# Scan products F, G and X as 64x64 quarters of the TensorE array

## The chip, the cores and the metric

The kernel runs on one core of one Trainium2 chip. Its engines work side by side and are tied together by semaphores: TensorE (PE: matmuls, with weight loads listed as PEld), VectorE (DVE), ScalarE (ACT), GpSimd (POOL) and SyncE (SP, which issues most DMAs). Each engine takes its instructions in order. The metric is the device time of one execution in microseconds; lower is better.

## The reference, cut to what matters

One layer of a bidirectional RWKV-7 / short-convolution hybrid: 128 context tokens and 2048 latent tokens, 1024 channels, one input and one output projection. The part that the change touches is the RWKV-7 state recurrence, 8 heads of 64 channels, run once forward and once backward:

```python
def step(S, inp):
    r_t, w_t, k_t, v_t, kk_t, a_t = inp
    s_kk = jnp.einsum('bdhij,bdhj->bdhi', S, kk_t)
    S = (S * w_t[..., None, :] - s_kk[..., :, None] * (kk_t * a_t)[..., None, :]
         + v_t[..., :, None] * k_t[..., None, :])
    return S, jnp.einsum('bdhij,bdhj->bdhi', S, r_t)

s_final, ys = lax.scan(step, s0.astype(f32), xs)
```

The kernel does not step token by token. It cuts the tokens into chunks of 64; within a chunk the recurrence becomes products of 64x64 matrices (one per head and direction), one of which needs a triangular inverse, and only one state of 64x64 goes from chunk to chunk.

## The kernel before

**Phases.** `phase1` normalises, projects, and writes to DRAM the scaled operands of the scan: per direction four arrays (called al, rh, ka, be in `OPS`) of 512 channels by 2176 tokens. `phase2` is the scan. `phase3` makes the output projection; part of it (`ahead`) runs inside the last scan stages.

**Stages.** `stages` has 17 entries (`NST`). A stage is two groups, `st.g[0]` the forward and `st.g[1]` the backward direction, each of 8 units; a unit is one chunk of 64 tokens of two heads (128 partitions: head 0 on partitions 0 to 63, head 1 on 64 to 127). The two heads of a unit have the same channels' place, but separate 64x64 matrices.

**Parts of a stage**, each a Python generator that emits instructions:

- `partL` (L853): loads the operands `rr` [128, 5, 8, 64] of both directions on SP's queue, two DMAs for each. Slot 2 of `rr` holds a constant identity. `rr` comes from a ring of two buffers.
- `partM` (L871), for one direction after the other: `make_bd` (L829) copies `rr` slot 0 and slot 4 into block-diagonal operands `pb` and `qb` (four ScalarE copies of 64x512). `product` (L888) makes four units' matmuls into one PSUM bank of the pool `O.pm` (two banks, tag "m") and evicts it on VectorE with a mask (L893). F and f are the two halves of the first product (slot 0 against slots 2 and 3), G and g those of the second (slot 4 against slots 1 and 0), Q the transposes of slot 4. The block-diagonal operand lets a 128x128 matmul treat both heads at once; the zeros in it keep them apart. D (`blocks`) takes 32x32 blocks out of GA with ScalarE and VectorE and sends them to DRAM (`at`) from ScalarE's queue.
- `partI` (L909): GpSimd loads `at` as `ab` (issued by SP), inverts the 32x32 triangular blocks by a loop of 15 rounds (L931, L934), and writes the result `zt` to DRAM (L935).
- `partW` (L955): copies and loads that fill the stacked operands `lt` and `rt`; loads `zt` back as `zc`. `partU` (L981): finishes the 64x64 inverse from the 32x32 blocks by products of 32x32 pieces (`psU` L992, `psW` L999) and builds `zb`, again block-diagonal, 128 wide.
- `partB` (L1011): X is `zb` against F (`psX`, L1018, pool `O.p2`, two banks, tag "s"), copied with a minus sign into `lt`/`rt` by ScalarE; then E is `lt` against `rt` (`psE`, L1029) with a mask on VectorE.
- `partS` (L1034): the chain itself, 8 steps: two matmuls a direction (`psS`, L1054), then VectorE scales the state into the next unit's `sv` (L1067).

**Order.** `main` (L1159) interleaves them: in stage s the steps of `partS(s)` are the frame; between them come pieces of W, U and B of stage s+1 (by `ORDER`) and pieces of `partM(s+3)` (`LA` = 3 stages ahead; by the tuple at L1204). `MORD` says which products make up one piece of `partM`. At the end of a stage come `partL(s+4)` and `partI(s+3)`. The tile framework then orders the instructions of each engine by a simulated time line, so that the order on the chip can differ from the order of emission; tiles of one tag share buffers in turn.

Of the kernel before, what the change touches and what calls it, by code (L numbers as in the profile page):

```python
# [681 lines left out]
MORD = ("Ff", "GgD", "", "Q")  # L682
# [8 lines left out]
def phase2(K):  # L691
# [4 lines left out]
    B = Ctx()  # L696
# [38 lines left out]
    def setup_rest():  # L735
# [21 lines left out]
        B.zb = O.l1.tile([128, 2, 8, 128], F32, name="zb")  # L757
# [113 lines left out]
    def partM(s, st):  # L871

        at = S["at"][s]
        for gi, g in enumerate(st.g):
            d = g.d
            rr = g.rr
# [5 lines left out]
            def transposes():  # L882
                pq = O.pm.tile([128, 4, 128], F32, tag="m", name=f"psQ{s}_{gi}")
                for k in range(4):
                    T.transpose(pq[:, k, :], rr[:, 4, 2 * k:2 * k + 2, :].rearrange("p u t -> p (u t)"), B.idt[:])
                copy("q", g.Q, pq[:])

            def product(h, dst, w, x, mask, nm):  # L888
                ps = O.pm.tile([128, 4, 128], F32, tag="m", name=f"ps{nm}{s}_{gi}_{h}")
                for i in range(4):  # L890
                    u = h * 4 + i
                    T.matmul(ps[:, i, :].rearrange("p (a b) -> p a b", b=64), w[:, u, :], x[:, :, u, :], start=True, stop=True)  # L892
                V.tensor_tensor(dst[:, h * 4:h * 4 + 4, :], ps[:], mask.unsqueeze(1).broadcast_to((128, 4, 128)), ALU.mult)  # L893

            def blocks():
# [7 lines left out]
            ops = dict(Q=transposes, F=lambda: F(0), f=lambda: F(1), G=lambda: GA(0), g=lambda: GA(1), D=blocks)  # L903
            for piece in MORD:
                for c in piece:
                    ops[c]()
                yield
# [47 lines left out]
    def partW(s, st):  # L955
# [5 lines left out]
        for n in range(2):  # L961
            for g in st.g:
# [18 lines left out]
    def partU(s, st):  # L981
# [7 lines left out]
        rows = [(slice(sl * 64, sl * 64 + 32), slice(sl * 64 + 32, sl * 64 + 64)) for sl in range(2)]  # L989
        for u in range(16):  # L990
            for r0, r1 in rows:
                T.matmul(pu[r1, u, :], st.g[u // 8].GA[r0, u % 8, 96:128], st.zr[r0, u, :], start=True, stop=True)  # L992
        for r0, r1 in rows:
# [3 lines left out]
        for u in range(16):  # L997
            for r0, r1 in rows:
                T.matmul(pw[r0, u, :], B.bu[r1, u, :], st.zc[r1, u, :], start=True, stop=True)  # L999
        zf = B.zb[:].rearrange("p d u c -> p (d u) c")  # L1000
        for r0, r1 in rows:
# [9 lines left out]
    def partB(s, st):  # L1011
        for n in range(2):
            for gi, g in enumerate(st.g):
                us = half(g, n)
                g.E.append(tl([128, 4, 2, 128], "E", 4))
                px = O.p2.tile([128, 4, 128], F32, tag="s", name=f"psX{s}_{gi}_{n}")
                for i in range(4):
                    T.matmul(px[:, i, :], B.zb[:, gi, us.start + i, :], g.F[:, us.start + i, :], start=True, stop=True)  # L1018
                for hd in range(2):
                    copy("x" if hd else "y", g.fs[64:128, :, hd, us], px[64 - hd * 64:128 - hd * 64].rearrange("p u (b t) -> p b u t", b=2), True)  # L1020
# [138 lines left out]
    def main():  # L1159
# [12 lines left out]
        for s in range(NST):  # L1172
# [30 lines left out]
            for i, _ in enumerate(partS(s, st, sts.get(s + 1))):  # L1203
                for _ in range((2, 2, 2, 1, 1, 0, 0, 0)[i]):  # L1204
# [209 lines left out]
```

## Time and profile before

| | us |
|---|---|
| time, median of 3 runs (lowest to highest) | 1759.63 (1756.57 to 1762.25) |
| span of the profiled execution | 1752.9 |
| first psS product of the scan, in that span | 1034.2 |
| last F product | 1458.6 |
| last X product | 1560.3 |

The profile gives one execution's span from its first to its last instruction; no separate device time of that execution is kept, so its span stands beside the median of the runs. Rows of groups read: line, engine, operation, output<-inputs, shape, xcount | busy us, mean ns of one | idle us of the engine just before, and what ended most of it. Matmul records carry the array rows*columns in use in front of the shape. A row of a time line reads: start us, length us, engine, line, operation, tiles, count, and in brackets the idle time ahead of it with what ended it.

### The profile page before, as it was taken

To read this page: it belongs to the slowest core of one execution; us is meant where nothing else is said; L and a number is where in the kernel's file an instruction comes from. 1 tells how busy PE (TensorE), PEld (TensorE's weight loads), DVE (VectorE), ACT (ScalarE), POOL (GpSimd) and SP (SyncE) were. 2 spreads that over 40 slices of the span, in tenths; PEclk is the share of its full clock that TensorE was granted. 3 is DMA by queue.
4 is the path that set the end of the run, shared out by engine and by line. 5 is a ranking of instruction groups with operands and counts; after the bars stand their busy time and mean duration, and the time that the engine had idled before them with its cause. 6 is when DMAs were issued, how large, how long until landed. Compare 5 with 4: busy or idle time off the path is not lost. (4 is left out here: it accounts for less than half of the span.)

```text
span 1752.9 us, 33041 instructions
## 1 busy us (share of the span) xinstructions
PE 1647.9 (94%) x12400; PEld 1558.8 (89%) x12400; DVE 1093.0 (62%) x2092; ACT 870.1 (50%) x1719; POOL 582.1 (33%) x1089
## 2 busy tenths in 40 slices
PE   5999899998999999999998989999999999899998
PEld 2889898998999998999998979899999999787886
DVE  5875788866567766567764544475776666656333
ACT  4534455534143433334442367687788787633222
POOL 0011111111011101011120587777777778223221
PEclk9899999999999999999999998899999999999999
DMA  9797778785557646477666585587677875746442
GB/s 367 208 234 220 233 241 246 232 255 151 148 160 227 169 147 174 135 258 217 195 214 225 173 196 135 141 192 187 174 198 189 191 185 120 180 151 206 151 144 90
DMA packets 315825, 335.69 MB, mean 192 GB/s; under 512 B 166985, under 2 KB 263881, under 8 KB 301585
## 3 DMA queue, kind: packets, MB, share of 16 engines
q1 hardware_dynamic: 243360, 324.52, 62.6%
q10 hardware_dynamic: 70944, 4.60, 2.9%
q0 software_dynamic: 1360, 4.46, 0.7%
q8 instruction: 98, 1.61, 0.4%
q14 instruction: 63, 0.51, 0.1%
HBM read 221.42 MB, written 112.08 MB: 190 GB/s over the span
## 5 line engine op out<-in xcount | busy, mean ns | idle before, releaser
L934 POOL TENSOR_TENSOR zt<-zt,ztmp 128x30 f32<-128x30 f32 (+7 forms) x510 | 197.3, 387 | 39.3
L1054 PE MATMUL psS<-sv,E 128*128 128x64 f32 x1088 | 155.1, 277 | 1.0 <-DVE sv L1067 0.6
L1029 PE MATMUL psE<-str,stl 128*128 128x128 f32 x1088 | 144.1, 281 | 11.3 <-DVE E L1030 7.0
L1054 PEld LDWEIGHTS psS<-sv,E 128*128 128x128 f32 x1088 | 145.4, 200 | 3.3 <-DVE sv L1067 0.8
L1029 PEld LDWEIGHTS psE<-str,stl 128*128 128x128 f32 x1088 | 131.8, 194 | 14.1 <-DVE E L1030 7.9
L931 POOL TENSOR_TENSOR ztmp<-ab,zt 128x60 f32<-128x60 f32 (+7 forms) x255 | 130.8, 513 | 19.2
L1067 DVE TENSOR_TENSOR sv<-psS,pc 64x128 f32<-64x128 f32 x254 | 69.2, 277 | 92.9 <-PE psS L1054 92.2
L779 ACT COPY bd<-rr 64x512 f32<-64x512 f32 x136 | 84.0, 617 | 75.7 <-DMA rr<-scr_ops 23.3
L323 POOL TENSOR_TENSOR shk<-rawl 128x384 f32<-128x384 f32 (+1 forms) x24 | 20.7, 861 | 291.9 <-ACT rawl L319 291.9
L1030 DVE TENSOR_TENSOR E<-psE,msk 128x512 f32<-128x512 f32 x136 | 92.7, 684 | 33.0 <-PE psE L1029 32.3
L892 PE MATMUL psF<-rr,bd 128*128 128x128 f32 x544 | 80.0, 295 | 16.2 <-ACT Q L779 9.8
L892 PEld LDWEIGHTS psF<-rr,bd 128*128 128x128 f32 x544 | 70.7, 203 | 20.4 <-ACT Q L779 12.9
L1350 POOL TENSOR_TENSOR z<-z,x 128x512 f32<-128x512 f32 x32 | 43.6, 1364 | 126.6 <-DVE z L1346 105.9
L1018 PE MATMUL psX<-F,zb 128*128 128x128 f32 x544 | 78.2, 297 | 3.2 <-ACT zb L777 2.3
L197 POOL TENSOR_TENSOR hslb<-kd,hshb 128x384 fp32r<-128x384 f32 (+1 forms) x24 | 26.7, 1113 | 164.0 <-ACT hshb L196 143.5
L160 PE MATMUL mmc<-h,w 128*128 128x384 f32 (+1 forms) x192 | 67.9, 354 | 13.4 <-ACT q1r L321 9.8
L323 POOL TENSOR_TENSOR shv<-rawl 128x384 f32<-128x384 f32 (+1 forms) x24 | 25.4, 1060 | 153.4 <-ACT rawl L319 153.4
L892 PE MATMUL psG<-rr,bd 128*128 128x128 f32 x544 | 72.0, 280 | 4.4 <-DVE F L893 4.4
L1018 PEld LDWEIGHTS psX<-F,zb 128*128 128x128 f32 x544 | 71.6, 209 | 4.0 <-POOL zt L934 1.9
L892 PEld LDWEIGHTS psG<-rr,bd 128*128 128x128 f32 x544 | 65.7, 193 | 5.0 <-DVE F L893 4.8
L161 PE MATMUL mmc<-h,w 128*128 128x384 f32 (+1 forms) x192 | 66.1, 344 | 0.0
L162 PE MATMUL mmc<-h,w 128*128 128x384 f32 (+1 forms) x192 | 65.7, 342 | 0.0
(307 smaller groups left out, 5205.4 us busy)
## 6 DMA issues: line engine op xcount, KB each, us to landing
w<-scr_wsp SPq DMA_DIRECT2D x68, 1024.0 KB, 7.3
scr_wsp<-w SPq DMA_DIRECT2D x34, 1024.0 KB, 6.0
rr<-scr_ops SPq DMA_DIRECT2D x64, 512.0 KB, 4.6
scr_ops<-sp SPq DMA_DIRECT2D x160, 192.0 KB, 5.2
wr<-in_win SPq DMA_DIRECT2D x34, 512.0 KB, 6.3
ab<-scr_at SPq DMA_DIRECT2D x34, 256.0 KB, 4.2
x<-in_x SPq DMA_DIRECT2D x17, 512.0 KB, 3.8
wadas<-in_wada SPq DMA_DIRECT2D x8, 1024.0 KB, 13.0
```

The costliest lines, as they stand in the source:

```text
L160: T.matmul(ps[:, :n], w[:, 0, k], hh[:, 0, k, :n], start=k == 0, stop=False)
L161: T.matmul(ps[:, :n], w[:, 0, k], hh[:, 1, k, :n], start=False, stop=False)
L162: T.matmul(ps[:, :n], w[:, 1, k], hh[:, 0, k, :n], start=False, stop=k == 7)
L779: (V.tensor_copy if k in ON_DVE else P.copy)(dst, src)
L892: T.matmul(ps[:, i, :].rearrange("p (a b) -> p a b", b=64), w[:, u, :], x[:, :, u, :], start=True, stop=True)
L931: G.tensor_tensor(tv, ab[:, j:j + 2, j + 2:32].unsqueeze(1).broadcast_to((128, kn, 2, n)), zt[:, :kn, j:j + 2].unsqueeze(3).broadcast_to(( ...
L934: G.tensor_tensor(zt[:, :kn, j + 2:32], zt[:, :kn, j + 2:32], tv[:, :, r], ALU.subtract)
L1018: T.matmul(px[:, i, :], B.zb[:, gi, us.start + i, :], g.F[:, us.start + i, :], start=True, stop=True)
L1029: T.matmul(pe[:, i, hd, :].rearrange("p (b t) -> p b t", b=2), g.lt[:, :, hd, us.start + k + i].rearrange("p b t -> p (b t)"), g.rt[:, :, ...
L1030: V.tensor_tensor(g.E[n][:, k:k + 2].rearrange("p a b c -> p (a b) c"), pe[:].rearrange("p a b c -> p (a b) c"), B.msk[:, ME[g.d]].unsquee ...
L1054: T.matmul(sp[gi][:, q, hd, :], g.E[n][:, k, hd, :], sv[:, u, hd, :], start=True, stop=True)
L1067: r = V.tensor_tensor(dst, sp[gi][0:64, q], B.pc[0:64, d, 2 * p:2 * p + 2, c:c + 1].broadcast_to((64, 2, 64)), ALU.mult)
```

## The change

F, G and X are no longer made with 128x128 operands. Each product of a unit is now two matmuls with 64 rows and 64 columns of the array, one per head, and the products of both directions are emitted alternately, so that four consecutive matmuls take the four 64x64 quarters. `place` says into which half of the partitions a head's result goes: crossed for the forward direction, as it was, and straight for the backward one. The two directions write two PSUM banks. The ring `bd`, `make_bd` and their copies are removed; `rr` gets a third buffer; `zb` becomes half as wide. `MORD` has six pieces for both directions together (there were four for each), with D following the second half of G for both directions and the two Q at the end; the pieces go one to each of the first six steps.

```diff
-MORD = ("Ff", "GgD", "", "Q")
+MORD = ("F", "f", "G", "gD", "Q", "q")
...
-        B.bd = ring(O.r1, 2, [128, 8, 128], "bd", zero)
-        B.rr = ring(O.r1, 2, [128, 5, 8, 64], "rr", presetR)
+        B.rr = ring(O.r1, 3, [128, 5, 8, 64], "rr", presetR)
...
-        B.zb = O.l1.tile([128, 2, 8, 128], F32, name="zb")
+        B.zb = O.l1.tile([128, 2, 8, 64], F32, name="zb")
...
-    def make_bd(t_, src):
-        copy("b", t_[0:64, :, 64:128], src[0:64])
-        copy("c", t_[64:128, :, 0:64], src[64:128])
+    def place(g, hd):
+
+        return 1 - hd if g.d == 0 else hd
+
+    def rows(i):
+        return slice(i * 64, i * 64 + 64)
...
-            pb, qb = B.bd(), B.bd()
-            make_bd(pb, rr[:, 0])
-            make_bd(qb, rr[:, 4])
...
-            def product(h, dst, w, x, mask, nm):
-                ps = O.pm.tile([128, 4, 128], F32, tag="m", name=f"ps{nm}{s}_{gi}_{h}")
-                for i in range(4):
-                    u = h * 4 + i
-                    T.matmul(ps[:, i, :].rearrange("p (a b) -> p a b", b=64), w[:, u, :], x[:, :, u, :], start=True, stop=True)
-                V.tensor_tensor(dst[:, h * 4:h * 4 + 4, :], ps[:], mask.unsqueeze(1).broadcast_to((128, 4, 128)), ALU.mult)
+        def product(h, w, xs, dst, mask, nm):
+            ps = [O.pm.tile([128, 4, 128], F32, tag="m", name=f"ps{nm}{s}_{gi}_{h}") for gi in range(2)]
+            for i in range(4):
+                u = h * 4 + i
+                for g, p_ in zip(st.g, ps):
+                    for hd in range(2):
+                        r = rows(hd)
+                        T.matmul(p_[rows(place(g, hd)), i, :].rearrange("p (a b) -> p a b", b=64), g.rr[r, w, u, :], g.rr[r, xs, u, :], start=True, stop=True)
+            for g, p_ in zip(st.g, ps):
+                V.tensor_tensor(dst(g)[:, h * 4:h * 4 + 4, :], p_[:], mask(g).unsqueeze(1).broadcast_to((128, 4, 128)), ALU.mult)
...
-            F = lambda h: product(h, g.F, pb, rr[:, 2:4], B.msk[:, MF[d]], "F")
-            GA = lambda h: product(h, g.GA, qb, rr[:, 1::-1], B.mkg[:, MG[d]], "G")
+        def F(h):
+            product(h, 0, slice(2, 4), lambda g: g.F, lambda g: B.msk[:, MF[g.d]], "F")
+
+        def GA(h):
+            product(h, 4, slice(1, None, -1), lambda g: g.GA, lambda g: B.mkg[:, MG[g.d]], "G")
...
+        def blocks():
+            for gi, g in enumerate(st.g):
...
-                    r = slice(64 - i * 64, 128 - i * 64)
-                    copy("g", g.gs[64:128, 1, i, us], g.GA[r, us, 0:64])
+                    copy("g", g.gs[64:128, 1, i, us], g.GA[rows(place(g, i)), us, 0:64])
...
-            for r in (r0, r1):
-                copy("z", zf[r, :, r], st.zc[r])
-            copy("n", zf[r0, :, r1], pw[r0], True)
+            for i, r in enumerate((r0, r1)):
+                copy("z", zf[r, :, i * 32:i * 32 + 32], st.zc[r])
+            copy("n", zf[r0, :, 32:64], pw[r0], True)
...
+            px = [O.p2.tile([128, 4, 128], F32, tag="s", name=f"psX{s}_{gi}_{n}") for gi in range(2)]
+            for i in range(4):
+                for gi, g in enumerate(st.g):
+                    u = half(g, n).start + i
+                    for hd in range(2):
+                        r = rows(place(g, hd))
+                        T.matmul(px[gi][rows(1 - hd), i, :], B.zb[r, gi, u, :], g.F[r, u, :], start=True, stop=True)
...
-                px = O.p2.tile([128, 4, 128], F32, tag="s", name=f"psX{s}_{gi}_{n}")
-                for i in range(4):
-                    T.matmul(px[:, i, :], B.zb[:, gi, us.start + i, :], g.F[:, us.start + i, :], start=True, stop=True)
...
-                for _ in range((2, 2, 2, 1, 1, 0, 0, 0)[i]):
+                for _ in range((1, 1, 1, 1, 1, 1, 0, 0)[i]):
```

More of the change, by code (lines that the diff above doesn't have):

```diff
@@ new lines, in F, with transposes @@
+        def F(h):
+            product(h, 0, slice(2, 4), lambda g: g.F, lambda g: B.msk[:, MF[g.d]], "F")
+        def GA(h):
+            product(h, 4, slice(1, None, -1), lambda g: g.GA, lambda g: B.mkg[:, MG[g.d]], "G")
+        def transposes(gi):
+            g = st.g[gi]
+            pq = O.pm.tile([128, 4, 128], F32, tag="m", name=f"psQ{s}_{gi}")
+            for k in range(4):
+                T.transpose(pq[:, k, :], g.rr[:, 4, 2 * k:2 * k + 2, :].rearrange("p u t -> p (u t)"), B.idt[:])
+            copy("q", g.Q, pq[:])
@@ L899, in blocks @@
                 nc.scalar.dma_start(at[gi * 8:gi * 8 + 8].rearrange("u s b j i -> (s b j) u i"), dg[:])
-            F = lambda h: product(h, g.F, pb, rr[:, 2:4], B.msk[:, MF[d]], "F")
-            GA = lambda h: product(h, g.GA, qb, rr[:, 1::-1], B.mkg[:, MG[d]], "G")
[L903 to L907, printed above, removed]
+        ops = dict(Q=lambda: transposes(0), q=lambda: transposes(1), F=lambda: F(0), f=lambda: F(1), G=lambda: GA(0), g=lambda: GA(1), D=blocks)
+        for piece in MORD:
+            for c in piece:
+                ops[c]()
+            yield
     def partI(s, st):
@@ L988, in partU @@
         pu = O.p2.tile([128, 16, 32], F32, tag="s", name=f"psU{s}")
-        rows = [(slice(sl * 64, sl * 64 + 32), slice(sl * 64 + 32, sl * 64 + 64)) for sl in range(2)]
+        parts = [(slice(sl * 64, sl * 64 + 32), slice(sl * 64 + 32, sl * 64 + 64)) for sl in range(2)]
         for u in range(16):
-            for r0, r1 in rows:
+            for r0, r1 in parts:
                 T.matmul(pu[r1, u, :], st.g[u // 8].GA[r0, u % 8, 96:128], st.zr[r0, u, :], start=True, stop=True)
-        for r0, r1 in rows:
+        for r0, r1 in parts:
             copy("u", B.bu[r1], pu[r1])
@@ L997, in partU @@
         for u in range(16):
-            for r0, r1 in rows:
+            for r0, r1 in parts:
                 T.matmul(pw[r0, u, :], B.bu[r1, u, :], st.zc[r1, u, :], start=True, stop=True)
         zf = B.zb[:].rearrange("p d u c -> p (d u) c")
-        for r0, r1 in rows:
-            for r in (r0, r1):
-                copy("z", zf[r, :, r], st.zc[r])
-            copy("n", zf[r0, :, r1], pw[r0], True)
+        for r0, r1 in parts:
+            for i, r in enumerate((r0, r1)):
+                copy("z", zf[r, :, i * 32:i * 32 + 32], st.zc[r])
+            copy("n", zf[r0, :, 32:64], pw[r0], True)
         yield
```

10 lines of the change are left out of this document (1 added, 9 removed).

## The prediction

> **What bounds the kernel now.** I began with the page's first part (busy time of each engine), then cut the scan into its 17 stages by the first psS product of each, read each stretch's busy times and clock, and last went through one stage in order of time. The window rows show the stretch, its length, busy us (and instructions) of PE, PEld, DVE, ACT and POOL, the granted TensorE clock, DMA share and GB/s.
>
> ```profile
> span 1752.9 us, 33041 instructions
> PE 1647.9 (94%) x12400; PEld 1558.8 (89%) x12400; DVE 1093.0 (62%) x2092; ACT 870.1 (50%) x1719; POOL 582.1 (33%) x1089
> ...
> 1034.20:1073.00 38.80, 35.52 (x363) 34.48 (x362) 16.27 (x36) 25.43 (x49) 29.26 (x66) 0.82 0.56 141
> 1103.70:1141.80 38.10, 34.64 (x362) 33.11 (x362) 19.04 (x42) 25.48 (x49) 31.11 (x72) 0.87 0.56 144
> 1201.30:1237.80 36.50, 34.67 (x367) 33.38 (x365) 20.84 (x42) 26.23 (x51) 27.25 (x64) 0.86 0.78 186
> 1267.40:1297.00 29.60, 29.41 (x366) 28.84 (x365) 21.61 (x43) 24.02 (x46) 22.86 (x51) 1.00 0.76 197
> 1420.20:1451.20 31.00, 29.58 (x366) 28.92 (x365) 20.01 (x43) 26.21 (x51) 25.48 (x56) 1.00 0.73 183
> ```
>
> Thirteen stages (1034 to 1451 us) run in full form. Three fell to a clock of 0.82 to 0.87 and took 38.8 + 38.1 + 36.5 = 113.4 us; the other ten kept 1.00 and took (1451.2 - 1034.2 - 113.4)/10 = 30.4 in the mean. A drop costs 113.4/3 - 30.4 = 7.4. In a good stage PE is busy 29.41 of 29.60 us. Whether that is real work is seen from the spacing of its instructions. In the stretches below: start, length, engine, line, tile written, count of records.
>
> ```profile
> 1277.08 2.00 PE L892 MATMUL psG<-rr,bd 128*128 128x128 f32 x16
> 1278.92 1.95 PE L1029 MATMUL psE<-str,stl 128*128 128x128 f32 x16
> 1281.99 1.06 PE L892 MATMUL psF<-rr,bd 128*128 128x128 f32 x8
> 1282.98 1.20 PE L992 MATMUL psU<-zr,GA 32*32 32x32 f32 x64
> 1284.11 1.10 PE L1054 MATMUL psS<-sv,E 128*128 128x64 f32 x8
> ...
> L1029 PE MATMUL psE<-str,stl x1088: 275/275/422, 1030.2 to 1566.6; 128*128 128x128 f32 x182
> L992 PE MATMUL psU<-zr,GA x1088: 191/191/258, 1017.4 to 1534.5; 32*32 32x32 f32 x182
> ```
>
> psE: 16 records start over 1.95 - 0.275 = 1.675 us, so one every 1.675/15 = 0.112 us. Each F, G, X, E and S product shows as two records, two passes (F: 17 stages x 2 directions x 8 units are 272 products; a row further down has 68 evictions of four). A full stage has 32 + 32 + 32 (F, G, X) + 64 (E) + 64 (S) = 224 records x 0.112 = 25.1 us, 12 transposes (psQ, psT) 1.3, psU and psW 1.1 each: 28.6 of 29.6 us. PE is the bound of a good stage, and only just.
>
> **What is next to bound.** GpSimd's triangular inversion (L919 to L935) is one unbroken run per stage; `zt` goes out by its own DMA, and the `zc` load waits for that.
>
> ```profile
> 1261.97 0.20 POOL L923 COPY dgp<-ab 128x16 f32<-128x16 f32 x1 [0.36 <-DMA ab<-scr_at]
> 1288.27 0.62 POOL L935 DMA_DIRECT2D scr_zt<-zt  x1 [0.30 <-POOL zt L934]
> 1291.82 0.20 POOL L923 COPY dgp<-ab 128x16 f32<-128x16 f32 x1 [2.94 <-DMA ab<-scr_at]
> ...
> POOL dgp L923 <- DMA ab<-scr_at: 30.2, 10, 7.6
> POOL zt L919 <- DMA scr_zt<-zt: 15.4, 6, 5.3
> SPq L978 <- DMA scr_zt<-zt: 40.3, 10, 9.2
> SPq L914 <- DMA scr_at<-dg: 29.6, 11, 4.9
> ```
>
> From the first row to the end of the second: 1288.89 - 1261.97 = 26.9 us, with only small gaps. The wait rows cover 1100 to 1480 us, 12.5 stages of 30.4. There GpSimd waits 30.2/12.5 = 2.4 us a stage for `ab`, which a faster PE delivers sooner, and 15.4/12.5 = 1.2 us for the previous `zt` to land, which it does not. So GpSimd stands at 26.9 + 1.2 = **28.1 us a stage**. The stage has 30.4; the headroom is 2.3 us, whatever PE saves.
>
> **The change, part by part.**
>
> *F, G and X as quarters.* Two products of the full array (four records, 0.448 us) become four 64x64 quarters (eight records). Do quarters run side by side? psU has 32x32 pieces in pairs that share neither rows nor columns: 64 records start over 1.20 - 0.191 us, 0.032 a pair. One alone, scaled from psE's 128 columns to 32, is 0.112/4 = 0.028. They do run together. The first stage of the program has four pieces on the same rows and four column groups:
>
> ```profile
> L190 PE MATMUL psrow<-wadas,scp 128*32 128x512 f32 x64 | 12.9, 890 | 10.5 <-DMA wadas<-in_wada 10.5
> ```
>
> One after another these would need 64 x 0.112 x 512/128 = 28.7 us; they took 12.9, much of it at half clock. Same columns from different rows, which the four quarters also need, no row shows. The bounds for one pass of four quarters: 0.112 (all together) and 0.448 (one by one), with 0.224 (two turns) between. I take 0.115, nearest to psU's: 0.032 against 0.028 is 0.004 of surcharge. A stage then needs 48 passes x 0.115 = 5.5 instead of 96 x 0.112 = 10.75 us: **5.2 us less PE**.
>
> *Changes of array shape.* From the rows above: the last psF starts at 1281.99 + 1.06 - 0.275 = 1282.78, psU at 1282.98, so 0.20 instead of 0.112; the last psU starts at 1283.99, psS at 1284.11, so 0.12 instead of 0.03. An excursion to small pieces costs 0.09 + 0.09 = 0.18 us. At least six new ones a stage (F twice, G twice, X twice); psS is now often put inside a group, which would make them 14 or so. I take eight: +1.5 us (1.1 to 2.6). PE after: 28.6 - 5.2 + 1.5 + 0.4 (psU's and psW's own) = **25.3 us**, under GpSimd's 28.1.
>
> *The bd copies go.* Half-width copies on ScalarE, and their zeroing:
>
> ```profile
> L779 ACT COPY bd<-rr 64x512 f32<-64x512 f32 x136 | 84.0, 617 | 75.7 <-DMA rr<-scr_ops 23.3
> L893 DVE TENSOR_TENSOR F<-psF,msk x68: 652/691/694, 945.2 to 1459.0; 128x512 f32<-128x512 f32 x68
> ```
>
> Eight a stage x 0.617 = 4.9 us off ScalarE's 24 to 26. It is not the bound and hides behind PE and GpSimd, so worth nothing in the sum, a shorter path from `rr` to F at most. Four `zb` copies a stage keep their size; DVE's F and G evictions keep count and size.
>
> *Both directions at once.* A product now fills both "m" banks (8 passes, 0.92 us), and the next needs both free: two evictions of 0.691, 1.4 us on DVE. One piece per step of the scan (a step is 30.4/8 = 3.8 us) leaves psS and psE to cover it; without cover it is 1.4 us x 4 a stage, and PE would still be at 25.3 + 5.6 = 30.9. X likewise takes both "s" banks ahead of four ScalarE copies, as many as before.
>
> *MORD, rr, dg.* The third `rr` buffer lets one direction's load (two of a stage's four SP-queue DMAs) go out a product set earlier; DMA bytes are the same. Two blocks in a row share one `dg` buffer, so the second ScalarE activation waits for the first's DMA: 29.6/11 = 2.7 us from the SP row, on a queue with the copies for E behind it and `at`, `ab`, GpSimd after it. With 4.9 us freed there it is covered; uncovered it lengthens a stage by up to 2.7.
>
> **The sum.** Thirteen stages x 2.3 = 29.9. Three late stages without F and G save on X alone: 32 x 0.112 - 16 x 0.115 - 2 x 0.18 = 1.4 each, 4. Ahead of the first stage one set of F and G (64 x 0.112 - 32 x 0.115 - 4 x 0.18 = 2.8) and its X (1.4) stand on the path to the scan: 4. Together 37.9. Against it I set one more drop of the clock, 7.4 (below). Span 1752.9 - 30.5 = 1722.4. This one execution gives no time beyond its span; the median of the three runs is 1759.6, 6.7 above it, and I take that as what lies around: **1729 us**.
>
> **The clock.** The slowest stages show what PE idling costs.
>
> ```profile
> 1214.40:1217.81 3.41, 3.41 (x44) 3.29 (x44) 1.87 (x5) 2.83 (x6) 2.94 (x7) 1.00 0.72 205
> 1217.81:1221.23 3.42, 2.01 (x70) 1.83 (x64) 1.24 (x4) 3.30 (x8) 2.87 (x8) 1.00 0.88 189
> 1221.23:1231.47 10.24, 10.19 (x100) 9.72 (x101) 3.53 (x6) 4.52 (x8) 4.96 (x12) 0.50 0.56 146
> ...
> 1217.59 1.20 PE L992 MATMUL psU<-zr,GA 32*32 32x32 f32 x64
> 1218.72 1.10 PE L1054 MATMUL psS<-sv,E 128*128 128x64 f32 x8
> 1221.28 2.08 PE L892 MATMUL psF<-rr,bd 128*128 128x128 f32 x8 [1.46 <-ACT Q L779]
> ```
>
> In 3.42 us PE did psU, which fills an eighth of the array, eight psS records, and stood 1.46 us; then the clock was 0.50 for 10.24 us. After the change PE streams (128 + 48) x 0.112 = 19.7 us in a stage of 28.1, 70% of it, against 25.1 of 30.4, 83%: such stretches get likelier.
>
> The Trainium skill (TensorE: Matmul & The Clock Gate, section "Why this matters for your kernels") asks only that PE not idle for more than about 3 us between bursts. By that rule there would be no more drops and the sum without my 7.4 would be 1722; the row differs, since 1.46 us next to small products was enough, and the row decides.
>
> **The rivals.**
> *Everything falls into place* (0.17): GpSimd's `zt` wait goes too, no stage loses its clock. Ten stages gain 30.4 - 26.9 = 3.5, the three slow ones 113.4 - 3 x 26.9 = 32.7, and 8 as above: 1752.9 - 75.7 + 6.7 = 1684. For it: the `zt` row has 6 waits in 12 stages. Against it: the clock.
> *The clock decides* (0.22, slower): in the psU and psW stretch of most stages PE waits for GpSimd and drops to 0.50. At 7.4 a drop, 37.9/7.4 = 5 more of them eat the gain; at eight it is 1752.9 - 37.9 + 59.2 + 6.7 = 1781. For it: the 70%. Against it: with GpSimd as the bound part of a drop is hidden.
> *The quarters take turns* (0.08, slower): two heads of a direction write one bank from different rows. At two turns, 0.224 a pass, nothing is saved and 1.5 us a stage is added: 1752.9 + 19.5 + 6.7 = 1779.
>
> The Trainium skill (TensorEngine Tiling, section "Gotcha 1: PSUM Pressure") says that different row tiles cannot access the same PSUM bank simultaneously. By that rule this third case would be the outcome; the trace disagrees, as psU's two pieces write one bank at 0.032 a pair.
>
> **How the numbers follow.** The forecast has 0.53, its own range 1707 (28.1 reached, no new drop and two of the three old ones gone: 1722 - 15) to 1751 (four new drops: 1722 + 29). Reaching into the other cases on both sides: 1688 to 1784. Within 0.3% is 5.3 us, about what this kernel's measurement can tell. Faster: 0.46 of the forecast and 0.17; same: 0.05 and 0.03 of the clock's; slower: the rest, 0.29.
>
> **What would show it.** Quarter groups: 16 products of F over two directions in about 0.92 us, four records starting together; if they start 0.11 apart, the quarters take turns. GpSimd: `dgp` no longer waiting for `ab`, stages at 28. ScalarE: no `bd` rows, 84 us less. Clock: the count of stages under 0.9; over eight, and the second rival holds. Wrong altogether if PE's idle before psF, psG or psX grows past 3 us a stage, waiting for DVE's or ScalarE's release of banks.

## The result, and the profile after

| | before | after |
|---|---|---|
| time, median (lowest to highest), us | 1760.94 (1756.57 to 1764.61) | 1859.30 (1855.73 to 1860.04) |
| span of the profiled execution, us | 1752.9 | 1857.5 |
| first psS product of the scan, us | 1034.2 | 1054.3 |
| the thirteen full stages, us | 417.0 | 499.6 |
| in them: no matmul running, us | 16.2 | 75.9 |
| in them: granted clock at 0.50, us | 34.1 | 116.1 |

The ratio of the times is 1.0547, with a 95% interval of 1.0522 to 1.0572: slower by 5.5%, outside the predicted range. Of the 104.6 us between the spans, 82.6 lie in the thirteen stages, 20.1 ahead of them and 1.9 behind. Of the 82.6, 59.7 are time without a matmul (75.9 less 16.2); by the other 22.9 matmuls ran longer.

The first part of the page of the changed kernel:

```profile
span 1857.5 us, 36323 instructions
PE 1668.8 (90%) x14032; PEld 1535.5 (83%) x14032; DVE 1087.0 (59%) x2093; ACT 778.2 (42%) x1583; POOL 580.9 (31%) x1087
```

Four of its thirteen stages, as stretches from one first psS to the next (columns as before):

```profile
1054.25:1092.70 38.45, 31.70 (x458) 28.39 (x457) 15.60 (x35) 19.89 (x41) 22.46 (x54) 0.91 0.55 137
...
1240.74:1283.41 42.67, 31.71 (x467) 28.52 (x466) 18.10 (x39) 19.43 (x40) 24.43 (x54) 0.84 0.53 135
...
1352.00:1381.28 29.28, 28.87 (x469) 26.05 (x467) 17.67 (x39) 20.07 (x41) 23.42 (x51) 1.00 0.58 137
...
1504.83:1553.87 49.04, 36.39 (x471) 31.89 (x469) 19.97 (x41) 21.68 (x45) 30.17 (x67) 0.79 0.46 103
```

ScalarE fell by 92 us, 84.0 of them its bd copies. PE's busy time did not fall at all, though F, G and X were to need half of theirs. The shortest stages are as long as good ones were before; the long ones show PE standing and half clock together. The next view is the waits of the changed kernel from 1100 to 1570 us (who waited for what: us in all, times, longest), first the engines, then SP's DMA queue.

```profile
POOL dgp L931 <- DMA ab<-scr_at: 87.9, 11, 14.9
...
POOL zt L927 <- DMA scr_zt<-zt: 32.6, 11, 5.0
...
PE psF L887 <- DMA rr<-scr_ops: 20.5, 3, 9.4
```

```profile
SPq L985 <- DMA scr_zt<-zt: 69.8, 10, 12.1
```

GpSimd's wait for `ab` has gone from 30.2 us to 87.9, the queue's wait for `zt` from 40.3 to 69.8. How these hang together is seen in one stage in order of time. The rows of PE, then those of SP, then those of GpSimd:

```profile
1255.30 1.10 PE L887 MATMUL psG<-rr 64*64 64x128 f32 x32
...
1266.44 0.44 PE L887 MATMUL psF<-rr 64*64 64x128 f32 x4
1275.12 1.56 PE L887 MATMUL psF<-rr 64*64 64x128 f32 x24 [8.24 <-issue]
1276.61 2.08 PE L1040 MATMUL psE<-str,stl 128*128 128x128 f32 x8
```

```profile
1256.43 0.88 SPq L870 DMA_DIRECT2D rr<-scr_ops  x2
1267.54 1.32 SPq L985 DMA_DIRECT2D zc<-scr_zt  x2
1268.96 0.60 SPq L1116 DMA_DIRECT2D sg<-scr_sg  x1
1269.66 0.38 SPq L870 DMA_DIRECT2D rr<-scr_ops  x1
1270.13 0.42 SPq L1152 DMA_DIRECT2D scr_mixT<-yo  x1
1270.64 0.38 SPq L1116 DMA_DIRECT2D w<-scr_q  x1
1271.11 0.44 SPq L870 DMA_DIRECT2D rr<-scr_ops  x1
1271.65 1.37 SPq L922 DMA_DIRECT2D ab<-scr_at  x2
```

```profile
1264.69 0.61 POOL L943 DMA_DIRECT2D scr_zt<-zt  x1 [0.30 <-POOL zt L942]
...
1280.32 0.20 POOL L931 COPY dgp<-ab 128x16 f32<-128x16 f32 x1 [12.01 <-DMA ab<-scr_at]
```

The rr load of a direction is two DMAs. Of the four in these rows, two go out at 1256.4; the other two stand in SP's queue behind `zc`, which waits until the `zt` that GpSimd sends at 1264.7 has landed, and go out at 1269.7 and 1271.1. PE has begun F and stands 8.24 us in front of the second direction's part, with psE and psS queued behind it. The row's `<-issue` names no cause, but the trace's semaphores do: PE's weight loads wait from 1265.98 to 1275.07 for one rr DMA of 1256.4 and for that of 1269.7, which landed at 1275.03. When PE goes on, psE takes 2.08 us for 8 records that took 1.16 us at 1250: half clock (0.50 is granted from 1267.5 to 1281.2). `ab` is issued last, GpSimd stands 12.0 us, so the next `zt` is late and with it the next `zc`. It is a loop over several engines and one queue.

The quarters themselves: the first PE row above has 32 records in 1.10 us, eight passes of four, as predicted. Earlier in the same stage stands the other half of G:

```profile
1247.68 1.08 PE L887 MATMUL psG<-rr 64*64 64x128 f32 x14
1248.69 1.16 PE L1040 MATMUL psE<-str,stl 128*128 128x128 f32 x8
1249.78 0.43 PE L887 MATMUL psG<-rr 64*64 64x128 f32 x2
1250.14 1.16 PE L1040 MATMUL psE<-str,stl 128*128 128x128 f32 x8
1251.23 1.08 PE L887 MATMUL psG<-rr 64*64 64x128 f32 x16
```

The same 32 records took 1.08 us twice, with entries into the small shape of their own: their records start mostly two at a time (1247.68 twice, 1247.84 twice, and so on), so only two quarters run side by side and half the array stands empty. Over the thirteen stages 27% of F's records, 56% of G's and 37% of X's start in groups of four, each within 0.045 us of the one before. The loop in `product` emits the directions alternately; that the tile framework's simulated time line put each direction where its own bank was free is an explanation, which the runs with one PSUM tile for both bear out below. Taking each record as 0.109 us from its start (twice that at half clock) and counting overlaps within F, within G and within X once, the three fill 9.2 us a stage after and 11.0 before. Fours throughout would be 5.2.

### The profile page after: what moved, and what is told of

Read it like the earlier page. It is cut to its first block, busy times and chain, and to the rows that moved or that the text cites. A ratio compares the mean times of both kernels' runs of the same rounds, so it can differ in the third digit from the quotient of the medians.

```text
span 1857.5 us, 36323 instructions
## 1 busy us (share of the span) xinstructions
PE 1668.8 (90%) x14032; PEld 1535.5 (83%) x14032; DVE 1087.0 (59%) x2093; ACT 778.2 (42%) x1583; POOL 580.9 (31%) x1087
## 4 chain that ended last, share of the span: by engine, by line
PE 49%; DMA 24%; DVE 12%; ACT 5%; issue 4%; POOL 4%; SPq 1%; DVEq 0%; ACTq 0%; POOLq 0%
DMA scr_ops<-sp 9%; PE psE L1040 7%; PE psS L1065 4%; DMA scr_at<-dg 3%; PE psu L1300 3%; PE psu L1298 3%; PE psu L1299 3%; PE psF L887 3%; DMA wr<-in_win 3%; PE psG L887 2%; POOL zt L942 2%; PE psX L1026 2%; DMA ab<-scr_at 1%; DMA rr<-scr_ops 1%; POOL ztmp L939 1%
## 5 line engine op out<-in xcount | busy, mean ns | idle before, releaser
L942 POOL TENSOR_TENSOR zt<-zt,ztmp 128x30 f32<-128x30 f32 (+7 forms) x510 | 202.0, 396 | 39.8
L1040 PE MATMUL psE<-str,stl 128*128 128x128 f32 x1088 | 174.7, 314 | 11.8 <-ACT str L776 7.8
L1040 PEld LDWEIGHTS psE<-str,stl 128*128 128x128 f32 x1088 | 153.4, 220 | 25.9 <-issue 8.1
L1065 PE MATMUL psS<-sv,E 128*128 128x64 f32 x1088 | 164.3, 284 | 11.3 <-DVE sv L1078 11.3
L1065 PEld LDWEIGHTS psS<-sv,E 128*128 128x128 f32 x1088 | 146.3, 201 | 30.2 <-issue 14.5
L887 PE MATMUL psF<-rr 64*64 64x128 f32 x1088 | 81.0, 318 | 72.5 <-DMA rr<-scr_ops 32.6
L939 POOL TENSOR_TENSOR ztmp<-ab,zt 128x60 f32<-128x60 f32 (+7 forms) x255 | 132.4, 519 | 19.7
L887 PEld LDWEIGHTS psF<-rr 64*64 64x64 f32 x1088 | 59.5, 154 | 81.9 <-issue 49.3
L889 DVE TENSOR_TENSOR F<-psF,msk 128x512 f32<-128x512 f32 x68 | 45.9, 683 | 53.7 <-PE psX L1026 27.4
L887 PE MATMUL psG<-rr 64*64 64x128 f32 x1088 | 65.4, 287 | 7.1 <-DVE F L889 7.1
L160 PE MATMUL mmgb<-h,w 128*128 128x384 f32 (+1 forms) x192 | 64.9, 338 | 1.2 <-DMA w<-scr_wsp 1.2
L162 PE MATMUL mmgb<-h,w 128*128 128x384 f32 (+1 forms) x192 | 64.6, 336 | 0.0
L161 PE MATMUL mmgb<-h,w 128*128 128x384 f32 (+1 forms) x192 | 64.3, 335 | 0.0
## 6 DMA issues: line engine op xcount, KB each, us to landing
wadas<-in_wada SPq DMA_DIRECT2D x8, 1024.0 KB, 12.8
```

Of the source, the lines that this page charges most:

```text
L160: T.matmul(ps[:, :n], w[:, 0, k], hh[:, 0, k, :n], start=k == 0, stop=False)
L161: T.matmul(ps[:, :n], w[:, 0, k], hh[:, 1, k, :n], start=False, stop=False)
L162: T.matmul(ps[:, :n], w[:, 1, k], hh[:, 0, k, :n], start=False, stop=k == 7)
L887: T.matmul(p_[rows(place(g, hd)), i, :].rearrange("p (a b) -> p a b", b=64), g.rr[r, w, u, :], g.rr[r, xs, u, :], start=True, stop=True)
L939: G.tensor_tensor(tv, ab[:, j:j + 2, j + 2:32].unsqueeze(1).broadcast_to((128, kn, 2, n)), zt[:, :kn, j:j + 2].unsqueeze(3).broadcast_to(( ...
L942: G.tensor_tensor(zt[:, :kn, j + 2:32], zt[:, :kn, j + 2:32], tv[:, :, r], ALU.subtract)
```

## The experiments

Three theories stood at the beginning. **The queue:** the loop above, with the second rr load as its start. **The order:** the pieces over six steps, with D fourth and Q last, make `at`, `ab` and the rr buffers late whatever the queue does. **The shared dg:** the second direction's D waits for the first's DMA. The fourth is **quarters in twos**: PE's work hardly falls. The runs of before in the same jobs had medians of 1758.2 to 1761.8 us; ratios go by those. The last three columns are from each one's trace, in us.

| kernel | time | ratio to before (95%) | 13 stages | no matmul | half clock |
|---|---|---|---|---|---|
| after | 1859.3 | 1.0547 (1.0522 to 1.0572) | 499.6 | 75.9 | 116.1 |
| spread222 | 1811.2 | 1.0293 (1.0253 to 1.0334) | 442.8 | 15.3 | 34.1 |
| gfirst | 1831.1 | 1.0412 (1.0371 to 1.0453) | 460.3 | 53.1 | 88.7 |
| gfirst_spread | 1791.6 | 1.0194 (1.0164 to 1.0223) | 425.4 | 22.6 | 20.5 |
| dg2 | 1853.3 | 1.0544 (1.0519 to 1.0569) | 476.3 | 59.1 | 85.3 |
| rr_act | 1823.1 | 1.0369 (1.0327 to 1.0412) | 458.5 | 37.3 | 78.5 |
| order_only | 1781.3 | 1.0128 (1.0085 to 1.0172) | 434.0 | 28.3 | 47.8 |
| onedir | 1780.1 | 1.0123 (1.0082 to 1.0163) | 427.3 | 13.4 | 6.8 |
| gs_dg2 | 1772.6 | 1.0073 (1.0050 to 1.0096) | 414.3 | 13.8 | 10.2 |
| gs_dg2_ztlate | 1772.2 | 1.0072 (1.0046 to 1.0098) | 418.1 | 14.2 | 17.1 |
| before_ztlate | 1758.8 | 0.9999 (0.9975 to 1.0023) | 421.8 | 19.7 | 37.5 |
| gs_dg2_pair | 1796.1 | 1.0190 (1.0151 to 1.0229) | 448.3 | 51.0 | 85.3 |
| after_pair | 1910.5 | 1.0842 (1.0796 to 1.0889) | 531.1 | 115.6 | 153.6 |
| gs_rr4 | 1766.5 | 1.0019 (0.9991 to 1.0047) | 414.5 | 17.2 | 10.2 |
| pair_rr4 | 1750.1 | 0.9945 (0.9916 to 0.9974) | 406.5 | 33.0 | 37.5 |
| pair_rr4_ztlate | 1727.4 | 0.9798 (0.9771 to 0.9825) | 383.1 | 20.2 | 10.2 |
| after_rr4 | 1836.4 | 1.0420 (1.0363 to 1.0477) | 466.0 | 51.3 | 81.9 |
| after_pair_rr4 | 1907.8 | 1.0842 (1.0779 to 1.0905) | 520.3 | 98.6 | 139.9 |

### Single edits of the changed kernel

**spread222**: the six pieces on three steps.

```diff
-                for _ in range((1, 1, 1, 1, 1, 1, 0, 0)[i]):
+                for _ in range((2, 2, 2, 0, 0, 0, 0, 0)[i]):
```

> The changed kernel with the pieces of a set of products (F, f, G, gD, Q, q) given two to each of the first three steps of the scan instead of one to each of six; nothing else is altered. Theory A (the set is made too late: rr is released late, at, ab and zt follow late, and the loads stand in line behind each other on SP's queue): under 1770 us, psF's wait for rr (32.6 us in the changed kernel) under 8, GpSimd's wait for ab down by more than half. Theory B (a product now needs both directions' rr and both banks, whatever its place): within 20 us of the changed kernel, 1840 to 1870. Theory C (the two blocks share one dg buffer and ScalarE stands for the first DMA): little change, 1835 to 1865, ScalarE's wait at dg as before.

It took 48 us off, a time that none of the three theories had. PE's idle time is back at the value of before, half clock too; GpSimd's wait for `ab` over 1100 to 1570 us falls from 87.9 to 47.0. What is left in the stages is PE's own time: the ten without a drop take 32.7 us in the mean, those of before 30.4.

**gfirst**: G and D ahead of F; **gfirst_spread**: both edits.

```diff
-MORD = ("F", "f", "G", "gD", "Q", "q")
+MORD = ("G", "gD", "Q", "q", "F", "f")
```

> The changed kernel with the order of pieces G, gD, Q, q, F, f: the blocks for GpSimd leave after the second step instead of the fourth, rr is still held to the sixth. Theory A1 (it is GpSimd's input that is late): 1740 to 1800 and GpSimd's wait for ab down by more than half. Theory A2 (it is the release of rr that is late): 1830 or more, since rr is released as late as before. Theory C: 1840 to 1865.

> Both edits: order G, gD, Q, q, F, f and two pieces to each of the first three steps. Theory A: the fastest of these, 1715 to 1760. Theory B: 1830 or more. Theory D (the lost time is the clock's: array share too low with quarters): clock drops stay as many, mean granted clock under 0.95 and 1800 or more.

28 us off alone, 68 together; 1831.1 is in the range of A2, and 1791.6 in none. In gfirst GpSimd still waits 79.7 us for `ab`, and PE waits for rr as well, here over 1100 to 1570 us:

```profile
PE psG L887 <- DMA rr<-scr_ops: 40.1, 12, 8.2
```

An early D alone doesn't bring `ab` in time. That fits A2: rr is held to the sixth step, and the next G starts late. Only with both edits does the wait for `ab` fall to 16.7.

**dg2**: two dg buffers.

```diff
-                dg = tl([128, 8, 32], "dg", 1, O.rI)
+                dg = tl([128, 8, 32], "dg", 2, O.rI)
```

> The changed kernel with two dg buffers instead of one; nothing else. Theory C: ScalarE's wait for the first block's DMA (41.7 us in 16 times) goes, at leaves 2.6 us earlier a stage, 1815 to 1835. Theory A: part of the lateness, 1830 to 1855. Theory B: no change, 1850 to 1865.

Six us between the medians and next to nothing between the ratios (1.0547 and 1.0544): the shared dg is not what makes the changed kernel slow. (On top of gfirst_spread the same edit took 19 us off, below: a wait decides only once the longer one ahead of it is gone.)

**rr_act**: the rr loads go out from ScalarE's queue, past `zc`.

```diff
-                    D(g.rr[:, i:i + 2].rearrange("p k u t -> p k (u t)"), src[k:k + 2].rearrange("k p t -> p k t"))
+                    nc.scalar.dma_start(g.rr[:, i:i + 2].rearrange("p k u t -> p k (u t)"), src[k:k + 2].rearrange("k p t -> p k t"))
```

> The changed kernel, order of pieces and steps as it has them; the two rr loads of each direction are issued from ScalarE's queue instead of SP's. Queue theory (rr stands on SP behind the loads that wait for zt and for E): psF's wait for rr falls from 32.6 us to under 10, GpSimd's wait for ab falls, 1790 to 1825. Rival (rr is simply released late by the sixth piece, whatever queue carries it): 1840 or more, psF's idle as before, now ScalarE stands as well.

36 us off, in the queue theory's range: the place behind `zc` costs that much, and it isn't all. GpSimd's wait for `ab` in this kernel still stands, 61.6 us over 1100 to 1570 us.

### Order and quarters apart

**order_only** takes the kernel before, with its full-array products, and gives it the changed order (its rr ring stays at two):

```diff
-MORD = ("Ff", "GgD", "", "Q")
+MORD = ("F", "f", "G", "gD", "Q", "q")
...
+                for g, p_ in zip(st.g, ps):
+                    T.matmul(p_[:, i, :].rearrange("p (a b) -> p a b", b=64), w(g)[:, u, :], g.rr[:, xs, u, :], start=True, stop=True)
```

**onedir** has the quarters, but one direction after the other as before, with the old order and steps; F and G can then fill two quarters at a time only.

```diff
+        for gi, g in enumerate(st.g):
+            def product(h, w, xs, dst, mask, nm):
...
+                    for hd in range(2):
+                        r = rows(hd)
+                        T.matmul(ps[rows(place(g, hd)), i, :].rearrange("p (a b) -> p a b", b=64), g.rr[r, w, u, :], g.rr[r, xs, u, :], start=True, stop=True)
```

> The kernel before with full-array, block-diagonal products (bd and rr rings of two, zb 128 wide, X as before), but the changed kernel's order: F and f of both directions, then G, gD, Q, q, one piece to each of the first six steps; the bd copies of slot 4 are made ahead of G. If the order alone makes the loss: 1820 to 1880. If the quarters make it (changes of array shape, clock): within 25 us of before, 1750 to 1785.

> The changed kernel with quarters, but the products of F and G made for one direction after the other, in the order and at the steps of before (Ff, GgD, none, Q; 2, 2, 2, 1, 1 pieces); two quarters run side by side, so F and G take TensorE as long as before, X half. Order theory: near before, 1740 to 1785 (X saves 1.8 us a stage, some 10 more changes of shape cost 1.8). Quarter theory: 1800 or more, though the order is the old one.

The order alone costs some 22 us, quarters with F and G in twos in the old order 21, and the whole change 98: they are worse in company. Each of the two times lies in the range that lays the loss on the other part, so neither part alone makes it. In onedir PE hardly idles and hardly drops; its twelve stages without a drop take 32.3 us in the mean instead of 30.4. Most of that is PE's own work: 13.2 entries into small shapes a stage instead of 2.9, at the 0.18 us of the prediction, are 1.9 us more, and F, G and X fill 10.5 us instead of 11.0, 0.5 less. The other 0.5 of the 1.9 us stays open.

### What holds the mended order

**gs_dg2** is gfirst_spread with two dg buffers: 1772.6 us.

> Order G, gD, Q, q, F, f, two pieces to each of the first three steps, and two dg buffers. Against 1791.6 without the second buffer: 6 us less as in the single edit (1780 to 1790) if the edits add; if at is now what GpSimd waits for, 10 to 20 less, 1770 to 1782. Not under before unless the start of the scan (27 us later in the span of the run without the buffer) comes forward too.

Its stages still take 31.4 us without a drop. The waits of gs_dg2 from 1060 to 1480 us:

```profile
POOL zt L927 <- DMA scr_zt<-zt: 39.2, 13, 3.6
POOL dgp L931 <- DMA ab<-scr_at: 11.8, 3, 4.4
```

GpSimd waits 3.0 us in every stage for the `zt` it has just sent, since the framework puts the next zeroing of `zt` right behind the sending. The theory was that GpSimd had become the bound. **gs_dg2_ztlate** ties the zeroing to the stage's own `ab`, and **before_ztlate** does so in the kernel before:

```diff
+        G.tensor_copy(zt[:, 0, 0:1], ab[:, 0, 0:1])
         G.memset(zt[:], 0.0)
```

> Order G D Q F, pieces on three steps, two dg buffers, and the zeroing of zt tied to its own stage by a one-column copy from ab ahead of it, so that it can no longer stand in GpSimd's queue right behind the sending of the zt before. Theory (with ab in time GpSimd's queue is the bound: 26.9 us of work and 3.0 us of waiting, 13 times in 13, for the zt just sent): the wait goes, GpSimd sends every 28 us instead of 31, the stages follow down to where PE or the clock holds them, 29 to 30: 1740 to 1755 us against 1772.6 without this edit. Rival (PE, its clock or the chain of psS holds the stage at 31 and GpSimd only waits because it has time): the wait moves to ab, stages stay at 31 to 32, 1768 to 1776.

> The kernel before with the same one-column copy ahead of the zeroing of zt, nothing else. Theory (PE's 28.6 us a stage and GpSimd's queue were about level there, GpSimd waiting for the zt just sent in half the stages): 0 to 1 us a stage, 1745 to 1762 us against 1760. Rival (GpSimd's wait was the bound before as well): 1725 to 1745. If this edit gives as much here as on the changed kernel, it says nothing on the change and what is left of the changed kernel's loss stays.

Both the same as without. In gs_dg2_ztlate the wait has only moved:

```profile
POOL zt L927 <- DMA ab<-scr_at: 49.2, 11, 9.1
```

So GpSimd waited because it had time; its queue was not the bound there, and the next suspect is PE's own work, which stands mostly in twos.

### Quarters in fours

**gs_dg2_pair** and **after_pair** give both directions one PSUM tile of two banks, so that neither direction can start alone; the transposes Q of both share one such tile too. X keeps its tiles.

```diff
-            ps = [O.pm.tile([128, 4, 128], F32, tag="m", name=f"ps{nm}{s}_{gi}_{h}") for gi in range(2)]
+            pb = O.pm.tile([128, 2, 4, 128], F32, tag="m", name=f"ps{nm}{s}_{h}", bufs=1)
+            ps = [pb[:, gi] for gi in range(2)]
```

> Order G D Q F, pieces on three steps, two dg buffers, and one PSUM tile of two banks for both directions, so that a product of F or G starts with both banks free and its quarters stand in fours (X stays as it is). Theory (with the waits gone PE's own work still sets the 31 us of a stage, because most quarters stand in twos: F, G and X occupy 9.3 us a stage there, where fours throughout would need 5.5): F and G fall from 6.3 to about 4 us a stage, some entries into small shapes go too, stages 28.5 to 29.5, 1735 to 1750 us against 1772.6 without it. Rival (PE is not the bound in this order; something that the trace calls busy is a wait for the chain of psS or for evictions): F and G fall, the time shows up between psS products, 1765 to 1778. Third (each product now waits for two evictions, 1.4 us of DVE, four times a stage): stages 32 to 34, 1780 to 1810.

> The changed kernel with that one edit alone (one PSUM tile of two banks for both directions; order, steps and dg as changed). Theory (the rr loads, ab and zt are late there whatever PE has to do): the loop of late loads stays, 1835 to 1860 us against 1859; less PE work may even bring the clock down more often. Rival (quarters in twos are the main loss of the change itself): 1800 or less.

Both got slower, by 24 and 51 us, though F did shrink. 1796 lies in the range of the third case, but not by its mechanism: PE's idle time before F is 2.1 us in all. 1911 lies above both ranges. F in gs_dg2, then the groups of gs_dg2_pair (busy, mean ns | idle ahead), and its waits from 1060 to 1480 us:

```profile
L887 PE MATMUL psF<-rr 64*64 64x128 f32 x1088 | 75.4, 285 | 1.4 <-ACT Q L778 1.4
```

```profile
L888 PE MATMUL psG<-rr 64*64 64x128 f32 x1088 | 73.2, 316 | 52.9 <-DMA rr<-scr_ops 46.3 <-issue 4.4 <-PE psS L1067 1.8
...
L888 PE MATMUL psF<-rr 64*64 64x128 f32 x1088 | 38.6, 276 | 2.1 <-DVE F L890 1.0 <-ACT Q L778 0.8
```

```profile
PE psG L888 <- DMA rr<-scr_ops: 33.0, 10, 9.7
```

F is at 38.6 us, against 75.4 in gs_dg2 and 81.0 in the changed kernel; 98% of its records start in fours. The five stages without a drop take 29.6. But psG, the first user of rr, now waits for its load, and its own time does not fall (71.5 us in gs_dg2). With both directions side by side both let go of their rr only at the end of the set; of three buffers one is ahead and the other load has to wait. The kernel before needed one rr at a time.

**pair_rr4** and **gs_rr4** have four rr buffers, made to fit by holding the identity once (64 columns) instead of eight times; **pair_rr4_ztlate** adds the copy ahead of the zeroing; **after_rr4** and **after_pair_rr4** have the four buffers with the order as changed.

```diff
-        B.rr = ring(O.r1, 3, [128, 5, 8, 64], "rr", presetR)
+        B.rr = ring(O.r1, 4, [128, 2112], "rr", presetR)
...
-        V.tensor_copy(t_[:, 2], i2b(8))
+        V.tensor_copy(t_[:, 0:64], B.I2[:])
```

> Quarters in fours (as gs_dg2_pair, 1796 us) and a fourth rr buffer, so that both directions' operands of the next set can be loaded while this set is still in use. Theory (a set that uses both directions side by side needs two pairs of rr; with three buffers the second load waits for the end of the set, PE waits for it and the clock drops): PE's wait for rr of 33 us goes, half-clock time falls from 85 to under 30 us, stages to 29 to 31, 1740 to 1765 us. Rival (the waits for both banks and the psS chain are what stall PE and halve the clock): 1785 to 1805, as before.

> The same with the zeroing of zt held behind ab (no wait for the zt just sent). Theory (with PE at 26 us GpSimd's queue, 26.9 + 0.6 + some 3 us of waiting for zt, is the bound of a stage): 1 to 2 us a stage less than pair_rr4, 15 to 25 us in all. Rival (PE or its clock is the bound still): within 5 us of pair_rr4, as this edit gave nothing on the other two kernels.

> Order G D Q F, three steps, two dg buffers, four rr buffers, quarters left to the scheduler (mostly in twos). Theory (rr was no longer late there: PE waited 3.6 us in all for it): 1768 to 1777 us, as gs_dg2 with 1772.6. Rival (the late second load still costs, through the places that the scheduler finds for it): 1755 to 1767.

> The changed kernel with four rr buffers, nothing else (F F G G+D Q Q over six steps, one dg buffer, quarters left to the scheduler). Theory (the second rr load, which stands behind zc on SP and waits for a buffer that is let go late, is the trigger of the loop; moving it to another queue gave 36 us): 1775 to 1815 us against 1859. Rival (the late D, so ab and GpSimd, is the loss whatever rr does): 1835 to 1860.

> The changed kernel with four rr buffers and one PSUM tile for both directions (quarters in fours), order, steps and dg as changed. Theory (with rr in time the fours save PE time; D in fourth place still makes ab late now and then): 1755 to 1800 us, 20 to 40 below after_rr4. Rival (with the order as changed, less PE work only lets the clock drop more often, as after_pair showed with 1911): above after_rr4.

| us | order as changed, six steps, one dg | G and D first, three steps, two dg |
|---|---|---|
| three rr, quarters as they fall | 1859.3 | 1772.6 |
| four rr | 1836.4 | 1766.5 |
| three rr, fours | 1910.5 | 1796.1 |
| four rr, fours | 1907.8 | 1750.1 |
| and the zeroing of zt late | not run | 1727.4 |

The right column bears the theory out. Fours with four rr are a little faster than before (ratio 0.9916 to 0.9974), though half-clock time, at 37.5 us, stays above the 30 expected. Then the zeroing of `zt`, worth nothing on two kernels, is worth 23 us, since PE now has room below GpSimd. GpSimd's wait at the zeroing from 1060 to 1480 us, in pair_rr4 and then in pair_rr4_ztlate:

```profile
POOL zt L929 <- DMA scr_zt<-zt: 43.5, 12, 6.3
```

```profile
POOL zt L929 <- DMA ab<-scr_at: 21.8, 6, 7.5
```

gs_rr4 came out in its rival's range, 6 us under gs_dg2. The left column shows that the rr ring is not the start of the loop by itself: a fourth buffer gives 23 us there, the rival's range, and fours make it worse. The waits from 1100 to 1570 us, of the engines and of SP's queue, first in after_rr4, then in after_pair_rr4:

```profile
POOL dgp L931 <- DMA ab<-scr_at: 75.3, 8, 14.7
```

```profile
SPq L985 <- DMA scr_zt<-zt: 102.0, 12, 16.6
```

```profile
POOL dgp L933 <- DMA ab<-scr_at: 129.0, 11, 15.1
```

```profile
SPq L987 <- DMA scr_zt<-zt: 187.2, 12, 20.9
```

With D in fourth place over six steps `ab` comes late whatever rr does, and less work on PE only means more standing: after_pair_rr4 has 98.6 us without a matmul and 139.9 us at half clock.

pair_rr4_ztlate ran 1726.7 to 1727.9 us in four runs. The head of its page, two of its thirteen stages, and one product of F for both directions on PE:

```profile
span 1726.1 us, 36371 instructions
PE 1602.2 (93%) x14032; PEld 1482.7 (86%) x14032; DVE 1083.8 (63%) x2094; ACT 776.9 (45%) x1583; POOL 580.9 (34%) x1104
```

```profile
1282.94:1310.54 27.60, 26.84 (x454) 24.53 (x453) 18.65 (x40) 20.72 (x43) 22.19 (x51) 1.00 0.69 186
...
1339.17:1367.13 27.96, 27.43 (x460) 24.72 (x459) 19.90 (x41) 17.32 (x36) 21.15 (x49) 1.00 0.95 199
```

```profile
1353.33 1.10 PE L888 MATMUL psF<-rr 64*64 64x128 f32 x32
```

Six of the thirteen stages take 27.1 to 28.0 us, just under the 28.1 that the prediction summed up; the mean is 29.5. That 1727.4 lies close to the forecast of 1729 is chance: this kernel has six edits more, and its F, G and X still fill 7.3 us a stage. Whether G first, four rr or two dg would have helped the full-array kernel as well was not tried; of the six edits only the zeroing was run there.

## Why the prediction was wrong

The forecast was 1729 us; it came to 1859. Step by step:

**Four quarters in 0.115 us a pass.** Right where four stand together: 32 records in 1.10 us, and no sign of the rival in which quarters take turns on the array.

**"A stage then needs 48 passes x 0.115 = 5.5 instead of 96 x 0.112 = 10.75 us: 5.2 us less PE."** The first step that failed. It took the order written in `product` for the order on PE. On PE most quarters went one direction at a time, by all that the runs with one PSUM tile show because each direction could start when its own bank came free, and F, G and X fill 9.2 us instead of 11.0: 1.8 less, not 5.2. The outcome of the third rival, quarters two at a time, came about in the order and not in the hardware. Shape changes took their 0.18 us each (0.205 us from start to start into the small shape and 0.199 out of it, against 0.112 between full-array records), but there were 12.8 a stage instead of 2.9, so 9.9 new ones, not eight: 1.8. The two cancel, so the gain that everything else was set against was about zero; the two stages without a drop took 31.5 and 29.3 us, where those of before had 30.4. The pair run shows this step: on the mended order F falls with fours from 75.4 to 38.6 us in all.

**"MORD, rr, dg" and "Both directions at once", costed at nothing but one direction's load that "goes out a product set earlier".** The step that made it slower. What decides is when D is done and when both rr are let go, and I costed neither. The sum's largest term, 13 x 2.3 us, took it that a faster PE delivers `ab` sooner; it came later, and GpSimd's wait for it went from 30.2 to 87.9 us. I named the dg wait as the danger there (2.7 us a stage); over 1100 to 1570 us it was 2.2 us, 12 times, and a second buffer gave 6 us.

```profile
ACT dg L907 <- DMA scr_at<-dg: 26.2, 12, 5.8
```

I had written down the two queue waits that grew (`zc` for `zt` on SP, GpSimd for `ab`) among the bounds, and did not ask what the moved rr load would stand behind. It stood behind `zc`. Putting D first and the pieces on three steps gives back 68 of the 98 us between the medians; moving the load to another queue alone 36; a fourth rr alone 23. They need not add: the fourth rr is worth 6 us on the mended order.

**GpSimd at 28.1 us a stage as the next bound.** Near the mark, but not reached in the changed kernel, whose stages took 38.4. In pair_rr4_ztlate, where the zeroing no longer waits for the `zt` before, nine of the first thirteen intervals between two sendings of `zt` are 26.8 to 28.5 us.

**One more clock drop, 7.4 us.** Half-clock time went from 34 to 116 us. By the test that I wrote down (more than eight stages under 0.9) the clock rival did not hold: five stages are, at 0.86, 0.87, 0.84, 0.77 and 0.79. In the stage shown the standing comes first: in the 3.41 us ahead of the drop at 1267.5 PE was busy 1.68 us, and the drop comes 0.65 us into the wait of 8.24. pair_rr4_ztlate has the small products too and 10 us at half clock. No run holds the clock fixed, so what half clock costs by itself is not shown; of the 82.6 us in the stages, matmuls ran 22.9 us longer, and as stages without a drop are about as long as before, that is an estimate of what it adds to their running time.

**The last test**, PE's idle before psF, psG or psX over 3 us a stage, came true: 72.5 us before psF over 17 sets, 4.3 each. But the largest part of it ends with rr's DMA, not with a release of banks.

```profile
L887 PE MATMUL psF<-rr 64*64 64x128 f32 x1088 | 81.0, 318 | 72.5 <-DMA rr<-scr_ops 32.6 <-ACT Q L778 11.4 <-DMA ab<-scr_at 10.9
```

**The 6.7 us around the span.** Most of that was the spread of single executions, not a fixed part: the profiled execution of after took 1859.28 us with a span of 1857.5, that of before_ztlate 1763.34 with 1761.6, so about 1.8 us lie around the span. The profiled execution of before was a short one, above all ahead of the scan: before_ztlate, changed on GpSimd alone, starts its first psS at 1042.9 instead of 1034.2. So 8.7 of the 20.1 us that the changed kernel loses there are not shown to be the change's. Why executions differ there stays open.

**"Ahead of the first stage" and "three late stages", 4 us saved each.** Neither came. From the first psF to the first psS it is 91.0 us in before, 89.1 in before_ztlate and 99.6 in after, so this stretch got 9 to 10 us longer; behind the thirteen stages 1.9 us were lost. What holds it up was not tried.

## What to carry to other kernels

Matmuls that are to run side by side on parts of the array have to become ready together: give them one PSUM tile and a full double buffer of operands, and look at the order on the engine rather than at the loop that emits them. Of every load that is moved, ask what waits at the head of its queue, and whether that wait depends, a stage later, on the load itself. What an edit is worth depends on the edits beside it: four rr and the late zeroing gave 6 and 0 us on the mended order, with fours 46 and 23.

## What was not expected of the hardware

Four 64x64 products that share columns in pairs ran at the rate of one (eight passes in 1.10 us), although two heads write one PSUM bank from different rows, into different partitions. The Trainium skill (TensorEngine Tiling, section "Gotcha 1: PSUM Pressure") says that different row tiles cannot access one bank at the same time; this trace disagrees.

Small products do not by themselves bring the clock down: onedir and pair_rr4_ztlate have 13.2 and 8.9 excursions a stage and 6.8 and 10.2 us at half clock in thirteen stages, against 34.1 for the kernel before with 2.9. What goes with half clock in these runs is standing: the kernels with over 50 us without a matmul have 82 to 154 us of it.
